# Weight chunks that begin at eight places in turn

## The chip, the cores and the metric

The kernel runs on one core of one Trainium2 chip. The metric is the device time in microseconds of one execution. Three runs of the kernel before took 3026.98, 3027.91 and 3037.3 us; the median is 3027.91 us.

## What is computed

Two transformer blocks of two layers each, one after the other, on 512 tokens of 1024 features; the first block has 256 context tokens beside them. All is in float32. In every layer the normalised input is multiplied by a wide input matrix, the products feed several mixers, and an output matrix closes the layer. Cut to what matters here, the first block is

```
h = rms_norm(x, g) * (1 + scale) + shift          # also for the context
qa, ka, va, za, qlb, kvlb, krb, zb, bc, cc, uc, zc, ga, gb, gc = split(h @ w_in)
ya = window_attention(qa, ka, va);  yb = latent_attention(qlb, kvlb, krb);  yc = bc * conv(cc * uc)
m  = sum over a, b, c of sigmoid(g) * ((y * silu(z)) @ w_branch)
x  = x + gate * rms_norm(m @ w_o, g_post)
```

and the second block

```
h = modulated rms_norm(x);  three mixers (attention, gated scan, attention) on split(h @ w_in)
x = x + gate * (mixers @ w_out)
h = modulated rms_norm(x);  u = conv(h @ w_up)     # 1024 -> 5632, 44 tiles of 128
x = x + gate * ((silu(u[:2816]) * u[2816:]) @ w_down)
```

## The kernel before

Features lie on the 128 partitions and tokens along the free dimension, so a feature tile is [128, 512] (with context [128, 768], as 512 and 256 columns). A matrix product runs tile by tile of its outputs: 128 output features at a time, over all feature tiles of the input.

Float32 products are made of two rounded parts: a number is a high part in float32r plus a low part in float32r, and `mm3` (line 174) adds up three products for each weight block of 128 x 128: high weights by high input, high weights by low input, low weights by high input. TensorE loads the block as its stationary operand and streams 512 or 256 columns of the input past it.

Weights come in chunks of 128 x 1024, eight blocks, through `wload` (line 149): SyncE issues the DMA of 512 KB into `wraw`, ScalarE casts it into the high part (`hi`, line 139), and VectorE subtracts to get the low part in pieces of 512 columns (`lo`, line 144). Most chunks go to the tiles `wh` and `wl`, two buffers of each, in the pool `wp`; these are the ones that the change touches:

```
h, l = (self.wp.tile([P, 1024], F32R, tag=t, name=self.nm(t), bufs=self.wb[1]) for t in ("wh", "wl"))
```

There are 364 of them. Chunks that have to stay longer, or that are loaded early, go to tiles of other pools (`w`, `mw`, `macc`, `w3`). In a chunk of 8 blocks of 128 columns block k lies 512 k bytes behind the chunk's start; in a chunk of 4 blocks of 256 columns 1024 k bytes.

The order of the work is that of the code, as a planner lays it out over the engines' queues; where a stream has gaps, steps of generators fill in (`Fill`). Names of outputs in the trace: `mm` the input projections, `pu` the branch products of the merge, `po` the output product of the first block, `up` and `dn` the second block's feed-forward (and `dn<-oh` its mixers' output product). Streamed tiles: `hh`, `hl` the normalised input (`ch`, `cl` its context columns), `yh`, `yl` the gated branches, `ah`, `al` the feed-forward's inner values, `oh`, `ol` the mixers' output.

Of the kernel before, what the change touches and what calls it, by code (L numbers as in the profile page):

```python
# [10 lines left out]
F32R = mybir.dt.float32r  # L11
# [5 lines left out]
P = 128  # L17
D = 1024
# [12 lines left out]
class Cat:  # L31
    """Column ranges of one feature tile kept in two tiles, split at column 512."""
# [10 lines left out]
class Pools:  # L43
    """Two pools as one: the tags named lie in the second."""
# [8 lines left out]
class Halves:  # L53
    """A chunk of weights in two tiles of 512 columns."""
# [13 lines left out]
class Fill:  # L68
    """Steps of generators, emitted a few at a time among the steps of another stream."""
# [34 lines left out]
class Kern:  # L104
    def __init__(self, ctx, tc, A):
        self.ctx, self.tc, self.nc, self.A = ctx, tc, tc.nc, A
        self.uid = 0
        self.ps = None
        self.fill = Fill()
# [39 lines left out]
    def wload(self, src, kt, n, tag=None):  # L149
        """A chunk [128, kt*n] of weights as an exact sum of two float32r parts."""  # L150
# [3 lines left out]
        if halves:  # L154
            h, l = (Halves([self.bp.tile([P, S], F32R, tag=tag, name=self.nm("w"), bufs=self.bb[tag]) for _ in range(2)], n) for _ in range(2))
        else:
            if tag:
                h, l = (self.bp.tile([P, 1024], F32R, tag=tag, name=self.nm(tag), bufs=self.bb[tag]) for _ in range(2))
            else:
                h, l = (self.wp.tile([P, 1024], F32R, tag=t, name=self.nm(t), bufs=self.wb[1]) for t in ("wh", "wl"))  # L160
# [13 lines left out]
    def mm3(self, ps, w, x, cols, n0=0, n1=P, ks=None, start=True, stop=True, o=0):  # L174
        """ps[n, t - o] += sum_k w[k][:, n] x[k][:, t] from split operands."""
# [9 lines left out]
    def seq(self, a, b):  # L185
        """Keeps b behind a in their engine's queue."""
        self.tc.add_manual_dep(b.ins, a.ins.name,
                               mybir.DependencyInfo(mybir.DependencyClass.NoSync, mybir.DependencyReason.DATA), reason="order")

    def after(self, ins):  # L190
        """Keeps ins behind the last product so far."""
# [3 lines left out]
    def rsqrt(self, v, n, inv, pool=True):  # L195
        """(v*inv + eps)^-0.5 of a small [128, n]: a first guess from the exponent, one step of third order, one of second."""
# [9 lines left out]
        # y * (15 - 10 a + 3 a^2) / 8  # L206
# [20 lines left out]
    def colsum(self, ps, a, nt):  # L227
        """ps[p, t] = sum over the partitions of a[:, t*128 + p]."""
# [3 lines left out]
    def rows(self, ps, r, nt):  # L232
        """ps[m, t*128 + p] = r[p, t] for every m."""
# [5 lines left out]
    def silu_cols(self, src, n, name, w):  # L239
        """[128, 8, w] with silu of n vectors in the first n columns, zeros elsewhere."""  # L240
# [13 lines left out]
    def mod_chunk(self, sc, n, wsrc, bias, layer, g, mt):  # L254
        """mt[:, 8g:8g+8, :] = 1024 outputs of s @ w + b for n vectors, on the tensor engine."""
# [12 lines left out]
    def mod_rows(self, ps, n, bias, g, mt):  # L268
        """Output 256j + c of vector r, in row 32j + r and column c of ps, to features on partitions, plus bias."""
# [6 lines left out]
        # feature g*1024 + j*256 + s*128 + p sits in column s*128 + j*32 + r  # L276
# [6 lines left out]
    def mod_steps(self, sc, n, wsrc, bias, layer, g, mt):  # L283
        """The same with the products on the vector engine; one step a 128 rows of w."""
# [19 lines left out]
    def mod_tile(self, name, bsrc, layer, nf, n):  # L304
        """Room for modulation vectors, and their biases."""
# [33 lines left out]
    def norm_part(self, xs, mod, g, c0, c1, j, ishift, iscale, dst, tmp=None, acc=None, sq="t"):  # L339
        """Columns c0:c1 of h = rms_norm(x, g) * (1 + scale) + shift, split into the tiles that dst(k) gives; mod  # L340
        [128, 24, n], of which column j. tmp(k): room for x times its gain, so that x itself is left intact; without it x is
        normalised in place, before the modulation is at hand. A step a feature tile."""
# [34 lines left out]
    def square(self, x, c0, c1, acc, tag="t"):  # L377
        """acc + x^2 of columns c0:c1, in a tile of its own."""
# [17 lines left out]
    def rms_rows(self, acc, w, inv):  # L396
        """(mean over the partitions' sum of acc + eps)^-0.5 of w columns, on every partition."""
# [14 lines left out]
    def h_x(self):  # L412
        """Room for h's first 512 columns: gives dst for norm_part."""
# [10 lines left out]
    def h_ctx(self):  # L424
        """The same for the columns from 512 on, of two feature tiles side by side."""
# [14 lines left out]
    def h_half(self, c):  # L440
        """The same for columns c*256 to (c+1)*256 of 512."""
# [11 lines left out]
    def norm_halves(self, mod, g, ishift, iscale, room):  # L453
        """h of self.x in two halves of the columns; room: makes tiles for x times its gain."""
# [13 lines left out]
    # tiles of w_in: qa 0-3 (x1 of two heads, x2 of both), ka 4, va 5, za 6-9, qlb 10-12, kvlb 13-14,  # L468
    # zb 15-18, bc 19-22, cc 23-26, uc 27-30, zc 31-34, ga 35-42, gb 43-50, gc 51-58
    def rope2(self, ps, tn):  # L470
        """Rotates the first 512 columns of rows x1 h0, x1 h1, x2 h0, x2 h1 (32 each); later columns pass through."""
# [13 lines left out]
    def a_kv(self, ps=None):  # L485
        """Keys of both groups with two copies of each part, and token-major values."""
# [23 lines left out]
    def a_q(self, p, tn, ps=None):  # L510
        """Queries of heads 2p, 2p+1: both rotary halves' high parts, then their low parts."""
# [15 lines left out]
    def pv_out(self, blocks, ecol, vst, y, row, q0):  # L527
        """y[row:row+64, q0:q0+256] = sum over key blocks of values times transposed weights, for two query tiles side by
        side in the array; blocks: [(key block, query tiles of the two)]."""
# [19 lines left out]
    def normalise(self, e, r):  # L549
        """e *= r, a factor a row."""  # L550
        self.nc.vector.tensor_scalar(e, e, r, None, op0=ALU.mult)  # L551

    def a_pair(self, h, q, i0, y):
        """Window attention of head h for query tiles i0, i0+1."""
# [41 lines left out]
    def ctx_pair(self, score, vst, y, row, scale, negmax, sink):  # L596
        """Attention of one head among the context tokens."""
# [34 lines left out]
    def attention(self, tn, conv):  # L632
        """Both attentions; projections that neither needs yet, and the gated convolution, fill in."""
# [61 lines left out]
    def latents(self, tn):  # L695
        """Queries of the first attention still to come, then the second's latents, rotary parts and first heads."""
# [7 lines left out]
        # keys and values  # L704
# [29 lines left out]
        # queries; their rms factor goes into the softmax's scale  # L734
# [25 lines left out]
        # shared rotary key: rows x1 x2 and, 32 further, x2 x1  # L760
# [12 lines left out]
        # rotary parts of all query heads, 16 rows a head  # L773
# [26 lines left out]
    def b_heads(self, tn, hp):  # L800
        """Q and K of heads 2hp, 2hp+1, unsplit: [96, T] with the rotary part in rows 64-95."""
# [30 lines left out]
    def b_vals(self, half):  # L832
        """Values of 4 heads, token-major: [128, 6, 2, 64] a pair of heads."""
# [73 lines left out]
    def gate(self, b, i, y, z0, tn):  # L907
        """y * silu(z), kept in DRAM until the merge."""
# [10 lines left out]
    def load_y(self, b, tn):  # L919
        """Split gated values of one branch."""  # L920
# [11 lines left out]
    def merge(self, bs, tn):  # L932
        """self.mh, self.ml = split sum over branches of sigmoid(g) * (y @ w_branch)."""
# [51 lines left out]
    def w_out(self, parts, mod, g_post, xsrc, tail):  # L985
        """x + gate * rms_norm(m @ w_o, g_post), in parts of the columns (first, last, column of mod); tail(i, xs) gives
        the steps that follow on part i, among which the next part's products run."""
# [31 lines left out]
    def post(self, os, xs, acc, c0, c1, behind):  # L1019
        """x += rms_norm(o) of columns c0:c1, acc the sums of o's squares."""  # L1020
# [29 lines left out]
    def block1(self):  # L1050
        """Both layers of the first block; the result is left in self.x, [128, 512] a feature tile, and the second block's
        first normalised input in self.hh, self.hl."""
# [99 lines left out]
    def next_h(self, i, xs, os, xd, mod, g):  # L1152
        """The second layer's normalised input; x itself goes to DRAM."""
# [26 lines left out]
    def cols2(self):  # L1180
        """The columns in one piece or, for the first products after a norm, in two."""
# [3 lines left out]
    def head_sums(self, st, sqs, ind, h0, nh):  # L1185
        """st[tok, t, h0:h0+nh] = sums of squares of nh heads, whose rows the columns of ind select."""
# [4 lines left out]
    def head_rows(self, r, h0, nh, rep):  # L1191
        """[128, 512] with r[tok, t, h] on the rep rows of each of the nh heads."""
# [7 lines left out]
    def values(self, ps, nh, name, tag="pt"):  # L1200
        """Token-major values of nh heads of 64: [128, 4, nh, 64]."""
# [10 lines left out]
    # tiles of w_in_2: A x1 of heads q0-3, A x1 of q4 q5 k0 k1, A x2 of both (0-3), av 4, bq 5-6, bff 7-8, bfb 9-10,  # L1212
    # bi 11-12, bg 13-14, cq 15-17, ck 18, cv 19
    def attn2_unit(self, q, ks, v, kv, soft, finish, y, row, i0):
        """Attention of one head for query tiles i0, i0+1 over all 512 tokens; soft(ps, i, j, e) leaves scores in e,
        finish(es) turns them to normalised weights."""
# [14 lines left out]
    def mix_done(self, i, y):  # L1231
        """Feature tile i of the mixers' output, split as soon as there is room beside the layer's input."""
# [8 lines left out]
    def room(self):  # L1241
        """The layer's input is not needed any longer."""
# [5 lines left out]
    def qk_split(self, q, t):  # L1248
        """The parts of the two heads of a tile of queries: high on the head's rows, low on the other's."""
# [9 lines left out]
    def k_split(self, k, t):  # L1259
        """High and low part of two heads' keys, each twice."""  # L1260
# [10 lines left out]
    def stats(self, ts):  # L1271
        """(mean square + eps)^-0.5 of the two heads of each tile: [128 tokens, 4, 2] a tile."""
# [8 lines left out]
    def a_prep(self):  # L1281
        """Queries and keys of the first mixer; the queries' rms factor goes into the softmax's scale."""
# [65 lines left out]
    def c_prep(self, tiles):  # L1348
        """Normalised queries, with the softmax's scale, or keys of the third mixer."""
# [20 lines left out]
    def stagger(*gens):  # L1370
        """The first steps of each generator run before the last one of the generator ahead of it."""
# [38 lines left out]
    def b_prep(self, pair):  # L1410
        """Of two heads: queries, values, and f, 1-f and log f, each [forward, backward], of the forget gates."""
# [455 lines left out]
```

## Time and profile before

| | |
|---|---|
| median of the runs | 3027.91 us |
| the profiled execution: its span, first to last instruction | 3026.6 us |
| TensorE products, busy | 2920.6 us (96%), 17920 |
| VectorE, ScalarE, GpSimd, busy | 1924.7, 1353.0, 261.5 us |
| mean granted TensorE clock, share of full speed | 0.986 |
| DMA | 331.76 MB, mean 110 GB/s |

The engines are named PE (TensorE's products), PEld (its weight loads), DVE (VectorE), ACT (ScalarE), POOL (GpSimd) and SP (SyncE). A product is pipelined: its duration reaches past the start of the next one, so the time that it takes out of a full stream is the distance of two starts. L182 is the line of `mm3` that issues the products.

### The profile page before, as it was taken

How to read it: one execution, taken by the hardware profiler on the slowest of the kernel's cores; microseconds unless marked ns; L12 is line 12 of the kernel's file. 1: busy time of each engine (PE TensorE's matmuls, PEld its weight loads, DVE VectorE, ACT ScalarE, POOL GpSimd, SP SyncE). 2: the span in 40 equal slices, each digit the busy share in tenths (PEclk: the TensorE clock that was granted, in tenths of full speed). 3: DMA queues.
4: the chain of work that ended last, by engine and by line, in shares of the span. 5: the costliest groups of instructions: out<-in, count | busy, mean ns of one | idle time of the engine just before them, and what ended most of it. 6: DMA issues, size and time to landing. Idle time of an engine off the chain costs nothing.

```text
span 3026.6 us, 46233 instructions
## 1 busy us (share of the span) xinstructions
PE 2920.6 (96%) x17920; PEld 2417.4 (80%) x17920; DVE 1924.7 (64%) x3720; ACT 1353.0 (45%) x2414; POOL 261.5 (9%) x520
## 2 busy tenths in 40 slices
PE   7999999999998999999998998999999998999999
PEld 4888888888887888777778876788888876788887
DVE  5666555555556566656676777688853778576642
ACT  3445544322234345653225775544433675554421
POOL 2000000001112000000112212000000223000000
PEclk9999999999998999999999999999999999999999
DMA  6221111333342423124653211355543311233232
GB/s 236 76 69 53 55 63 64 116 127 124 119 160 85 126 80 106 52 69 174 232 201 132 76 47 48 105 177 200 189 142 115 97 43 53 85 100 97 98 107 89
DMA packets 113163, 331.76 MB, mean 110 GB/s; under 512 B 18160, under 2 KB 20720, under 8 KB 112944
## 3 DMA queue, kind: packets, MB, share of 16 engines
q1 hardware_dynamic: 112944, 328.81, 33.6%
q8 instruction: 141, 2.31, 0.3%
q14 instruction: 78, 0.64, 0.1%
HBM read 300.51 MB, written 17.76 MB: 105 GB/s over the span
## 4 chain that ended last, share of the span: by engine, by line
PE 84%; DVE 8%; ACT 2%; DMA 2%; issue 2%; POOL 2%; SPq 0%; DVEq 0%; ACTq 0%; POOLq 0%
PE mm L182 32%; PE up L182 15%; PE dn L182 11%; PE pu L182 5%; PE pv L544 4%; PE pt L539 4%; PE po L182 2%; PE s L851 2%; PE s L568 1%; PE s L1223 1%; DVE zz L1527 1%; DVE wl L144 1%; PE pre L182 1%; PE pq L182 1%; DMA yg<-yd 1%
## 5 line engine op out<-in xcount | busy, mean ns | idle before, releaser
L144 DVE TENSOR_TENSOR wl<-wraw,wh 128x512 fp32r<-128x512 f32 (+2 forms) x706 | 473.1, 709 | 391.3 <-ACT wh L139 382.8
L139 ACT CAST wh<-wraw 128x1024 fp32r<-128x1024 f32 (+4 forms) x364 | 365.8, 1005 | 754.2 <-PE mm L182 241.5
L182 PE MATMUL mm<-hh,wh 128*128 128x512 f32 (+1 forms) x1240 | 488.8, 397 | 9.2 <-ACT hh L373 3.5
L182 PE MATMUL mm<-hl,wh 128*128 128x512 f32 (+1 forms) x1240 | 487.9, 394 | 5.0 <-DVE hl L374 5.0
L182 PE MATMUL mm<-hh,wl 128*128 128x512 f32 (+1 forms) x1240 | 487.3, 393 | 0.0
L182 PEld LDWEIGHTS mm<-hh,wh 128*128 128x128 f32 x1240 | 235.0, 191 | 58.2 <-ACT wh L139 6.9
L182 PEld LDWEIGHTS mm<-hl,wh 128*128 128x128 f32 x1240 | 235.8, 190 | 50.3 <-DVE hl L374 7.0
L182 PEld LDWEIGHTS mm<-hh,wl 128*128 128x128 f32 x1240 | 235.5, 190 | 49.6 <-DVE wl L144 3.0
L182 PE MATMUL up<-hh,wh 128*128 128x512 f32 (+1 forms) x688 | 261.1, 381 | 3.8 <-DVE fu L1643 2.3
L182 PE MATMUL up<-hl,wh 128*128 128x512 f32 (+1 forms) x688 | 261.0, 380 | 0.5
L182 PE MATMUL up<-hh,wl 128*128 128x512 f32 (+1 forms) x688 | 261.2, 380 | 0.2 <-DVE wl L144 0.2
L541 ACT COPY pT<-pt 128x512 f32<-128x512 f32 (+1 forms) x304 | 159.5, 551 | 177.0 <-PE pt L539 175.7
L294 DVE SCALAR_TENSOR_TENSOR macc<-mw,sc,macc 128x1024 f32<-128x1024 f32 x140 | 181.0, 1308 | 74.1 <-DMA mw<-w_mod 38.8
L539 PE MATMUL pt<-ident,E 128*128 128x128 f32 x1120 | 174.7, 282 | 4.1 <-DVE E L551 3.4
L539 PEld LDWEIGHTS pt<-ident,E 128*128 128x128 f32 x1120 | 127.8, 142 | 39.6 <-issue 24.4
L182 PEld LDWEIGHTS up<-hh,wh 128*128 128x128 f32 x688 | 128.8, 188 | 30.2 <-ACT ah L139 2.7
L182 PEld LDWEIGHTS up<-hl,wh 128*128 128x128 f32 x688 | 129.1, 188 | 26.2 <-DVE hl L374 1.3
L182 PEld LDWEIGHTS up<-hh,wl 128*128 128x128 f32 x688 | 129.1, 188 | 25.8 <-DVE wl L144 0.9
L964 POOL TENSOR_TENSOR m<-m,gt 128x768 f32<-128x768 f32 (+1 forms) x32 | 54.5, 1704 | 1077.4 <-DVE gt L960 755.8
L182 PE MATMUL mm<-ch,wl 128*128 128x256 f32 x504 | 143.7, 285 | 0.0
L182 PE MATMUL mm<-cl,wh 128*128 128x256 f32 x504 | 143.2, 284 | 0.0
L182 PE MATMUL mm<-ch,wh 128*128 128x256 f32 x504 | 143.1, 284 | 0.0
(416 smaller groups left out, 6135.7 us busy)
## 6 DMA issues: line engine op xcount, KB each, us to landing
wraw<-w_in SPq DMA_DIRECT2D x158, 512.0 KB, 3.5
mw<-w_ada SPq DMA_DIRECT2D x96, 512.0 KB, 4.4
wraw<-w_up SPq DMA_DIRECT2D x88, 512.0 KB, 3.5
mw<-w_mod SPq DMA_DIRECT2D x32, 512.0 KB, 3.5
wraw<-w_down SPq DMA_DIRECT2D x32, 512.0 KB, 3.5
wraw<-w_branch SPq DMA_DIRECT2D x24, 512.0 KB, 3.7
wraw<-w_out SPq DMA_DIRECT2D x22, 512.0 KB, 3.5
wraw<-w_o SPq DMA_DIRECT2D x19, 512.0 KB, 3.7
```

Of the source, the lines that this page charges most:

```text
L139: self.nc.scalar.copy(out, in_)
L144: (eng or self.nc.vector).tensor_tensor(out, in_, hi.bitcast(F32), op=ALU.subtract)
L182: self.last = self.nc.tensor.matmul(ps[: n1 - n0, c0 - o:c1 - o], lhsT=a[:, k, n0:n1], rhs=b[j][:, c0:c1], start=start and i == 0, stop=st ...
L294: nc.vector.scalar_tensor_tensor(acc[r], w, sc[:, k, r:r + 1], acc[r], op0=ALU.mult, op1=ALU.add)
L539: nc.tensor.transpose(pt[:, o * P:o * P + P], ecol(j, kb), self.ident)
L541: nc.scalar.copy(tt[:, :n], pt[:, :n])
L544: nc.tensor.matmul(pv[64 * j:64 * j + 64, :P], lhsT=vst(kb), rhs=tt[:, o * P:o * P + P], start=i == ends[j][0], stop=i == ends[j][-1])
L568: nc.tensor.matmul(s[:, c0:c1], lhsT=q[:, i * P:(i + 1) * P], rhs=kp[:, a0:a0 + c1 - c0], start=pi == 0, stop=pi == 1)
L851: self.nc.tensor.matmul(ps, lhsT=a[:96, i * P:(i + 1) * P], rhs=b[:96, c0:c1], start=pi == 0, stop=pi == 2)
L964: nc.gpsimd.tensor_tensor(ms[n][:, :tn], ms[n][:, :tn], m[:, :tn], op=ALU.add)
L1223: nc.tensor.matmul(s, lhsT=q[:, i * P:(i + 1) * P], rhs=kp, start=pi == 0, stop=pi == 1)
L1527: self.nc.vector.tensor_tensor(z[rows, h].rearrange("p (b u x) -> p b u x", u=2, x=H), q[rows].rearrange("p (b u x) -> p b u x", u=2, x=H) ...
```

## The change

The tiles `wh` and `wl` become 64 elements (256 bytes) longer. A counter goes round through 1 to 7 and 0, and a chunk begins 8 elements (32 bytes) times the counter behind its tile's start; both parts of a chunk have the same place. All that reads and writes the chunk goes by the slice. Chunks in other tiles stay as they were. Docstrings and comments are replaced by empty lines. The core of the diff:

```diff
@@ class Kern, __init__
-        self.uid = 0
+        self.uid, self.wturn = 0, 0
@@ wload
             if tag:
                 h, l = (self.bp.tile([P, 1024], F32R, tag=tag, name=self.nm(tag), bufs=self.bb[tag]) for _ in range(2))
             else:
-                h, l = (self.wp.tile([P, 1024], F32R, tag=t, name=self.nm(t), bufs=self.wb[1]) for t in ("wh", "wl"))
+
+                self.wturn = (self.wturn + 1) % 8
+                h, l = (self.wp.tile([P, 1024 + 64], F32R, tag=t, name=self.nm(t), bufs=self.wb[1])[:, 8 * self.wturn:8 * self.wturn + 1024]
+                        for t in ("wh", "wl"))
```

## Rows read from the trace of the kernel before

**Rows 1.** The page: span, busy time of each engine, the chain that ended last.
```profile
span 3026.6 us, 46233 instructions
...
PE 2920.6 (96%) x17920; PEld 2417.4 (80%) x17920; DVE 1924.7 (64%) x3720; ACT 1353.0 (45%) x2414; POOL 261.5 (9%) x520
...
PE 84%; DVE 8%; ACT 2%; DMA 2%; issue 2%; POOL 2%; SPq 0%; DVEq 0%; ACTq 0%; POOLq 0%
```

**Rows 2.** Waits of TensorE: waiter, waited for, us in total, times, longest.
```profile
PE mm L182 <- ACT wh L139: 3.3, 4, 1.0
...
PE po L182 <- DVE wl L144: 2.6, 1, 2.6
```

**Rows 3.** Products grouped by form: shape, count, busy us, mean ns, idle before.
```profile
L182 PE MATMUL mm<-hh,wh 128*128 128x512 f32 x1208 | 481.3, 400 | 8.1 <-ACT wh L139 3.3 <-ACT hh L373 2.4 <-DVE m L960 2.0
...
L182 PE MATMUL up<-hh,wl 128*128 128x512 f32 x624 | 243.5, 390 | 0.0
...
L182 PE MATMUL mm<-ch,wl 128*128 128x256 f32 x504 | 143.7, 285 | 0.0
...
L182 PE MATMUL dn<-ah,wl 128*128 128x512 f32 x330 | 130.2, 395 | 0.0
...
L182 PE MATMUL pu<-yl,wh 128*128 128x512 f32 x192 | 75.7, 394 | 0.0
...
L182 PE MATMUL dn<-oh,wl 128*128 128x256 f32 x160 | 45.4, 285 | 0.0
```

**Rows 4.** Timeline of TensorE in the up projection: start, us, first and last of seven.
```profile
2749.74 0.39 PE L182 MATMUL up<-hh,wl 128*128 128x512 f32 x1
...
2751.10 0.39 PE L182 MATMUL up<-hh,wl 128*128 128x512 f32 x1
```

**Rows 5.** The same in the down projection, first and last of seven.
```profile
2949.73 0.39 PE L182 MATMUL dn<-ah,wl 128*128 128x512 f32 x1
...
2951.13 0.39 PE L182 MATMUL dn<-ah,wl 128*128 128x512 f32 x1
```

**Rows 6.** Windows, two of up, one of down: us, PE busy (products), clock, DMA.
```profile
2700.00:2800.00 100.00, 100.00 (x443) 1.00 0.30 96
2800.00:2900.00 100.00, 100.00 (x442) 1.00 0.31 98
2910.00:3010.00 100.00, 100.00 (x430) 1.00 0.37 110
```

**Rows 7.** Timeline, 256 columns, mixers' output product, first and last of eight.
```profile
1932.75 0.28 PE L182 MATMUL dn<-oh,wh 128*128 128x256 f32 x1
...
1933.59 0.28 PE L182 MATMUL dn<-ol,wh 128*128 128x256 f32 x1
```

**Rows 8.** Timeline, 256 columns, weights in w, first and last of nine.
```profile
1975.86 0.28 PE L182 MATMUL up<-hh,w 128*128 128x256 f32 x1
...
1976.77 0.28 PE L182 MATMUL up<-hh,w 128*128 128x256 f32 x1
```

**Rows 9.** Timeline, 256 columns, streamed tile mh, first and last of eleven.
```profile
1611.81 0.28 PE L182 MATMUL po<-mh,w 128*128 128x256 f32 x1
...
1613.00 0.28 PE L182 MATMUL po<-ml,w 128*128 128x256 f32 x1
```

**Rows 10.** Timeline: first and last product behind which a pitch was read.
```profile
47.70 0.39 PE L182 MATMUL mm<-hh,wh 128*128 128x512 f32 x1
...
2899.34 0.39 PE L182 MATMUL up<-hh,wl 128*128 128x512 f32 x1
```

**Rows 11.** Timeline behind a wait: first, eighth and eleventh of eleven products.
```profile
1421.62 0.39 PE L182 MATMUL mm<-hh,wh 128*128 128x512 f32 x1
...
1423.23 0.39 PE L182 MATMUL mm<-hl,wh 128*128 128x512 f32 x1
...
1423.91 0.39 PE L182 MATMUL mm<-hl,wh 128*128 128x512 f32 x1
```

**Rows 12.** The second block's attention scores by line: count, ns min/median/max, first, last.
```profile
L1223 PE MATMUL s<-kl,qa x96: 387/394/797, 1708.6 to 2600.8; 128*128 128x512 f32 x96
```

## The prediction

> **What bounds the kernel now.** I read the page first. TensorE is busy 2920.6 us of the span of 3026.6 us, and the chain that ended last is TensorE for 84% of the span, with the products of line 182 at its head [rows 1]. So a change matters here if it makes a product shorter or longer, or if it makes TensorE wait. The waits come next: the longest that TensorE has for the split of a weight chunk are a few us in total [rows 2]. ScalarE and VectorE split the chunks ahead of need, and what the change does to their writes has room. The grouped instructions show where the time is: three products a weight block, of 512 columns for the most part [rows 3].
>
> The reader is then to look at the pitch, from start to start of two products, and not at the duration, for products overlap. In the up projection of the second layer six pitches of 512 columns take 2751.10 - 2749.74 = 1.36 us, 226.7 ns each [rows 4]. In the down projection six take 2951.13 - 2949.73 = 1.40 us, 233.3 ns [rows 5]. Both streams run with no gap, at a granted clock of 1.00, the upper level of 2.4 GHz, and the counts of whole windows agree: 442 or 443 products in 100 us against 430 [rows 6]. At that clock 512 columns at one a cycle would be 213.3 ns (an estimate from the clock); so 13.3 ns a product are lost in the one and 20 ns in the other.
>
> The two stretches are the same code with the same weight tiles. What differs is where the streamed tile lies. In the compiled kernel before, the weight tiles begin at multiples of 4096 bytes of a partition and their blocks follow at 512 (or 1024) bytes; hh and hl begin at multiples of 2048; ah and al begin 64 bytes past a multiple of 128. While one product streams, the next weights are loaded beside it. I call the place of those weights less the place of the tile then streamed, modulo 128 bytes, the distance: 0 in the up projection, 64 in the down projection.
>
> Three more stretches speak of the distance. At 256 columns and distance 0, seven pitches take 0.84 us, 120 ns each [rows 7]. At 256 columns with weights 64 bytes off and the streamed tile aligned, eight take 0.91 us, 113.8 ns [rows 8]. At 256 columns with the streamed tile 96 past (distance 32), ten take 1.19 us, 119 ns, with single ones between 115 and 123 [rows 9]. So weights off by 64 helped a short product and a streamed tile off by 64 hurt a long one: the place matters, and its sign isn't the same for both lengths.
>
> **The change, part by part.** It adds no instruction, DMA, wait or queue step. It gives each chunk in wh and wl a start 32 times 0 to 7 bytes into its tile, so that the distance of its products runs through 0, 32, 64, 96 and again. The tiles grow by 256 bytes, four of them, 1024 bytes a partition; tiles behind them move by that, a multiple of 128, and keep their distance to everything else. Chunks in other tiles (w, mw, macc, w3) stay.
>
> First term, 512 columns at distance 0. Counted are mm 3 x 1208, up 3 x 624 and pu 3 x 192, together 6072 [rows 3]. The timeline's starts give 6053 pitches of such products under 250 ns, the first at 47.70 us and the last at 2899.34 us [rows 10]: mean 228.0 ns, 78% of them at 226 to 228. The others stand behind a wait: there seven pitches take 1423.23 - 1421.62 = 1.61 us, 230 ns each, before the pitch settles at 0.68 / 3 = 226.7 [rows 11]. Three of four chunks leave distance 0: 0.75 x 6053 = 4540 products.
> - At 64 I take 233.3, as in the down projection.
> - At 32 and 96 no steady stretch of 512 columns exists. From below: 220.0, one step of 6.7 ns under 226.7, as the short product gained (120 to 113.3). From above: 240.0, a step over 233.3. The nearest row is the attention's second product, whose streamed tile lies 64 past and whose weights 96 past: its median duration is 394 ns [rows 12], as long as a product of the down projection (394 to 395) and longer than one of the up projection (390) [rows 3]. Unsettled pitches behind a wait are 230. I take 232.5.
> - Mean of the three: 232.8. Cost 4540 x 4.8 ns = 21.8 us; ends 4540 x (224.4 - 228.0) = -16 us and 4540 x (237.8 - 228.0) = +44 us.
>
> Second term, the down projection: 3 x 330 = 990 products at distance 64 [rows 3]. A quarter comes to distance 0 and gains 6.7 ns (-1.7 us), half goes to 32 or 96 (-0.4 us at 232.5). Together -2 us; ends -8 and +2.
>
> Third term, 256 columns: ch and cl 3 x 504, oh and ol 3 x 160, together 1992 [rows 3]; three quarters, 1494, leave distance 0. At 120 now; 113.8 at 64 and 119 at 32 and, taken alike, 96: 117.3 on average, 2.7 ns less, -4 us; ends -9 (all at 113.8) and 0.
>
> Fourth term: a stream that today stays settled from chunk to chunk is thrown out at each new place. The chunks that come to distance 0 settle anew; seven pitches 3.3 ns above 226.7 are 23 ns, for a quarter of some 360 chunks 2 us.
>
> Fifth term, writes: the cast into wh and the subtraction into wl begin at the same multiples of 32 bytes. Nothing that the trace shows depends on that; they stay hidden as long as TensorE's waits for them stay at a few us [rows 2]. Were each of 364 casts 0.05 us longer, it would be 18 us on ScalarE, busy 45% [rows 1]. I take 0.
>
> Sum: 21.8 - 2 - 4 + 2 = 17.8 us of TensorE. It stands idle 106 us in all (3026.6 - 2920.6), and where it waits for others a slower product uses up some of the wait; I take off a tenth: 16 us. The profiled execution's span of 3026.6 becomes 3042.6; the median of the runs is 3027.9, 1.3 us more than that span, so 3044.
>
> Here the Trainium skill speaks against any effect. Its page "SBUF — State Buffer", section "Who interferes with whom", gives TensorE two read ports, one for the streamed operand and one for weights, independent of each other, and says that TensorE never waits on anyone. By that rule the sum would be 0 and the time 3028; the 6.7 ns between the two projections at one clock would then have to come from the streamed tile alone, which is the second rival.
>
> **Rivals.**
> 1. Distances 32 and 96 cost no more than 0, or only half of the step: the first term is then 4540 x (228.9 - 228.0) = +4 us at 226.7, or 4540 x (231.1 - 228.0) = +14 at 230, and with the rest 3026 to 3038: no change that can be told. For it: at 256 columns distance 32 lies between 0 and 64. Against: the 394 ns of the attention.
> 2. Only the place of the streamed tile counts, and the place of the weights doesn't. The time stays 3028. For it: up and down differ in nothing but the streamed tile. Against: at 256 columns the streamed tile is aligned in both stretches, and weights moved by 64 changed 120 to 113.8.
> 3. Faster: the loss of 13.3 ns a product is itself a collision of two reads that start at the same place, and places apart remove it, as for the short products with moved weights. With 220.0 at 32 and 96 it is -16 - 8 - 9 + 2 = -31 us, some 2998. It decides for faster by 0.5% once the mean of the shifted distances is under about 227 ns. Against: the one steady stretch of 512 columns off distance 0 is slower.
> 4. Both odd distances cost a further step (240.0): +44 + 2 + 0 + 2 = 48 us, 3076.
>
> **How the numbers follow.** The forecast (232 to 234 at 32 and 96) has 0.48, rival 1 has 0.25, rival 2 has 0.12, rival 3 has 0.11, rival 4 has 0.04. The forecast's own range is 3036 to 3054, from 230.5 to 234.5 with a pass-through between 0.8 and 1; about a seventh of it lies under 3043, which is 0.5% over the time before, about what a measurement of this kernel can tell from no change. So slower 0.45, same 0.44, faster 0.11. The range of 8 in 10 reaches over the rivals 1 and 2 and a little into 3: 3012 to 3056.
>
> **What would show it.** Right: in the up projection the pitch alternates by chunk, a quarter at 226.7 and the rest at 232 or more; in the down projection a quarter falls to 226.7; the counts of 100 us windows come to about 432 in both; the granted clock and the order of the instructions are as before. Wrong: the up projection stays at 226.7 throughout (rival 2), or goes below it in some chunks (rival 3), or TensorE shows longer waits for wh and wl, which no term of mine has.

## The result and the profile after

Four runs of the changed kernel took 3045.05 to 3049.03 us, median 3047.75; the kernel before, run beside it, 3028.86. The ratio is 1.0058, with a 95% interval of 1.0045 to 1.0071: slower by about 0.6%, 18.9 us between the medians. The forecast was 3044. The profiled execution took 3049.03 us, its span is 3047.3 us, 20.7 us over that of before, at the same mean clock of 0.986.

The page after, with the lines that answer to [rows 1]:

```profile
span 3047.3 us, 46233 instructions
...
PE 2943.4 (97%) x17920; PEld 2417.1 (79%) x17920; DVE 1925.1 (63%) x3720; ACT 1351.0 (44%) x2414; POOL 261.7 (9%) x520
...
PE 84%; DVE 8%; ACT 2%; DMA 2%; issue 2%; POOL 2%; SPq 0%; DVEq 0%; ACTq 0%; POOLq 0%
```

The count of instructions, the chain and the work of the other engines are as before; only TensorE is busy longer, by 22.8 us. Lines of the code lie three further down, so L182 is now L185. The waits for split weights, against [rows 2]:

```profile
PE po L185 <- DVE wl L144: 2.6, 1, 2.6
...
PE mm L185 <- ACT wh L139: 2.3, 3, 1.0
```

They have not grown. The products grouped by form, against [rows 3]:

```profile
L185 PE MATMUL mm<-hh,wh 128*128 128x512 f32 x1208 | 485.6, 403 | 7.6 <-DVE m L963 2.5 <-ACT hh L376 2.4 <-ACT wh L139 2.3
...
L185 PE MATMUL up<-hh,wl 128*128 128x512 f32 x624 | 246.5, 395 | 0.0
...
L185 PE MATMUL mm<-ch,wl 128*128 128x256 f32 x504 | 142.7, 283 | 0.0
...
L185 PE MATMUL dn<-ah,wl 128*128 128x512 f32 x330 | 130.3, 395 | 0.0
```

Up takes 395 ns a product instead of 390, mm 403 instead of 400, the down projection 395 as before, and 256 columns 283 instead of 285. Windows of 100 us, two of up and one of down (us, PE busy and products, clock, DMA), against [rows 6]:

```profile
2720.00:2820.00 100.00, 100.00 (x432) 1.00 0.29 95
2820.00:2920.00 100.00, 100.00 (x432) 1.00 0.29 94
2930.00:3030.00 100.00, 100.00 (x433) 1.00 0.35 111
```

The up projection fell from 443 to 432 products, the down projection rose from 430 to 433, all at a granted clock of 1.00. Next the timeline in the up projection, against [rows 4]: the first product of six chunks in a row, 24 products apart.

```profile
2742.61 0.39 PE L185 MATMUL up<-hh,wh 128*128 128x512 f32 x1
...
2748.21 0.40 PE L185 MATMUL up<-hh,wh 128*128 128x512 f32 x1
...
2753.72 0.40 PE L185 MATMUL up<-hh,wh 128*128 128x512 f32 x1
...
2759.31 0.39 PE L185 MATMUL up<-hh,wh 128*128 128x512 f32 x1
...
2764.76 0.39 PE L185 MATMUL up<-hh,wh 128*128 128x512 f32 x1
...
2770.35 0.40 PE L185 MATMUL up<-hh,wh 128*128 128x512 f32 x1
```

These chunks lie 160, 192, 224, 0 and 32 bytes into their tiles. Divided by 24 the steps are 233.3, 229.6, 232.9, 227.1 and 232.9 ns. So the pitch does change from chunk to chunk, as forecast; but one chunk of eight has the old pitch, not one of four, and the chunk at 192 has a value of its own, although 192 and 64 are the same modulo 128.

Over the whole kernel, with the starts of the trace and the places of the compiled program, the mean pitch of 512 columns by distance modulo 256 bytes is 228.1 (0), 233.0 (32), 233.3 (64), 233.8 (96), 232.5 (128), 233.3 (160), 229.8 (192) and 233.2 (224); 829 to 961 pitches stand behind each.

### The profile page after: what moved, and what is told of

The parts are those of the page before. It is cut to its first block, busy times and chain, and to the rows that moved or that the text cites. A ratio compares the mean times of both kernels' runs of the same rounds, so it can differ in the third digit from the quotient of the medians.

```text
span 3047.3 us, 46233 instructions
## 1 busy us (share of the span) xinstructions
PE 2943.4 (97%) x17920; PEld 2417.1 (79%) x17920; DVE 1925.1 (63%) x3720; ACT 1351.0 (44%) x2414; POOL 261.7 (9%) x520
## 4 chain that ended last, share of the span: by engine, by line
PE 84%; DVE 8%; ACT 2%; DMA 2%; issue 2%; POOL 2%; SPq 0%; DVEq 0%; ACTq 0%; POOLq 0%
PE mm L185 32%; PE up L185 16%; PE dn L185 10%; PE pu L185 5%; PE pv L547 4%; PE pt L542 4%; PE po L185 2%; PE s L854 2%; PE s L571 1%; PE s L1226 1%; DVE zz L1530 1%; DVE wl L144 1%; PE pq L185 1%; PE pk L185 1%; PE kr L185 1%
## 5 line engine op out<-in xcount | busy, mean ns | idle before, releaser
L185 PE MATMUL mm<-hh,wh 128*128 128x512 f32 (+1 forms) x1240 | 493.4, 401 | 8.6 <-ACT hh L376 3.5
L185 PE MATMUL mm<-hl,wh 128*128 128x512 f32 (+1 forms) x1240 | 492.8, 398 | 5.3 <-DVE hl L377 5.3
L185 PE MATMUL mm<-hh,wl 128*128 128x512 f32 (+1 forms) x1240 | 492.6, 398 | 0.0
L185 PEld LDWEIGHTS mm<-hh,wh 128*128 128x128 f32 x1240 | 235.4, 191 | 61.0 <-ACT wh L139 5.7
L185 PEld LDWEIGHTS mm<-hl,wh 128*128 128x128 f32 x1240 | 236.7, 191 | 54.1 <-DVE hl L377 6.8
L185 PEld LDWEIGHTS mm<-hh,wl 128*128 128x128 f32 x1240 | 236.4, 191 | 53.8 <-DVE wl L144 3.0
L185 PE MATMUL up<-hh,wh 128*128 128x512 f32 (+1 forms) x688 | 263.9, 385 | 2.3 <-ACT wh L139 1.1
L185 PE MATMUL up<-hl,wh 128*128 128x512 f32 (+1 forms) x688 | 264.0, 385 | 0.5
L185 PE MATMUL up<-hh,wl 128*128 128x512 f32 (+1 forms) x688 | 264.1, 385 | 0.0
L185 PEld LDWEIGHTS up<-hh,wh 128*128 128x128 f32 x688 | 128.8, 188 | 31.6 <-ACT hh L376 1.6
L185 PEld LDWEIGHTS up<-hl,wh 128*128 128x128 f32 x688 | 129.1, 188 | 29.5 <-DVE hl L377 1.3
L185 PEld LDWEIGHTS up<-hh,wl 128*128 128x128 f32 x688 | 129.1, 188 | 28.2 <-issue 0.8
L185 PE MATMUL mm<-ch,wl 128*128 128x256 f32 x504 | 142.7, 283 | 0.0
L185 PE MATMUL mm<-ch,wh 128*128 128x256 f32 x504 | 142.4, 283 | 0.0
L185 PE MATMUL mm<-cl,wh 128*128 128x256 f32 x504 | 142.3, 282 | 0.0
```

The costliest lines, as they stand in the source:

```text
L185: self.last = self.nc.tensor.matmul(ps[: n1 - n0, c0 - o:c1 - o], lhsT=a[:, k, n0:n1], rhs=b[j][:, c0:c1], start=start and i == 0, stop=st ...
```

## The experiments

**The pitch by itself.** A small kernel without the network, of bare products: 48 products in a row for each pair of places, in the order of `mm3`. The weights lie w bytes and the streamed tile x bytes behind the starts of their tiles. In the compiled program all these starts lie 128 bytes past a multiple of 256, so w less x is the distance modulo 256; the places themselves are 128 bytes off from those of wh, wl, hh and hl in the big kernel, which begin at multiples of 256. The core of the edit (places are in elements of 4 bytes):

```diff
+    for n in (512, 256):
+        for d in range(0, 32, 2):
+            run(f"w{4 * d:03d}x000n{n}c", n, d, 0)
+        for wp, xp in ((0, 16), (16, 16), (8, 8), (0, 8), (0, 24), (0, 0), (32, 0), (0, 32)):
+            run(f"w{4 * wp:03d}x{4 * xp:03d}n{n}e", n, wp, xp)
```

> A kernel of its own: no network, only streams of 48 products of 128x128 weights, three a weight block as in the big kernel, at chosen places of the weights (w, bytes) and of the streamed tile (x, bytes), 512 and 256 columns; its output isn't the reference's. Theory D (the distance of the next weights from the streamed tile, modulo 128 bytes, sets the pitch): at 512 columns 226.7 ns at w000x000, w064x064, w032x032, w128x000 and w000x128; 233.3 at w000x064 and w064x000; between 231 and 235 at distances 32 and 96; at 256 columns 120 at distance 0, 113.3 to 117.7 at 64, about 118.4 at 32 and 96. Theory A (only the streamed tile's place counts): all w...x000 alike at 226.7, and w064x064 and w000x064 alike at 233.3. Theory W (only the weights' place counts): w064x064 like w064x000.

Timeline of this kernel; each name holds w, x and the columns, and of each pair stand the 18th and the 48th product, 30 pitches apart. The granted clock is 1.00 throughout (20 to 400 us):

```profile
27.76 0.39 PE L36 MATMUL w000x000n512c<-xha,wla 128*128 128x512 f32 x1
...
34.56 0.39 PE L36 MATMUL w000x000n512c<-xha,wla 128*128 128x512 f32 x1
...
71.61 0.40 PE L36 MATMUL w032x000n512c<-xha,wla 128*128 128x512 f32 x1
...
78.61 0.40 PE L36 MATMUL w032x000n512c<-xha,wla 128*128 128x512 f32 x1
...
194.67 0.39 PE L36 MATMUL w120x000n512c<-xha,wla 128*128 128x512 f32 x1
...
201.47 0.39 PE L36 MATMUL w120x000n512c<-xha,wla 128*128 128x512 f32 x1
...
216.57 0.39 PE L36 MATMUL w064x064n512e<-xha,wla 128*128 128x512 f32 x1
...
223.37 0.40 PE L36 MATMUL w064x064n512e<-xha,wla 128*128 128x512 f32 x1
...
271.78 0.39 PE L36 MATMUL w128x000n512e<-xha,wla 128*128 128x512 f32 x1
...
278.74 0.40 PE L36 MATMUL w128x000n512e<-xha,wla 128*128 128x512 f32 x1
```

That is 6.80 us / 30 = 226.7 ns at distance 0, 7.00 / 30 = 233.3 at 32, 226.7 at 120, 226.7 with both 64 off, and 6.96 / 30 = 232 at 128. The other steps of 8 bytes lie between 230.0 and 234.3; weights at 0 with the streamed tile at 64 give 228.9. Two things follow. The streamed tile at 0 gives 226.7 or 233.3 by where the weights lie, so rival 2 of the prediction is false; and with both moved alike the pitch is that of distance 0, so it is the difference of the two that counts. Distance 0 gives 226.7 here as in the big kernel, though both places are 128 bytes off from there. And 128 is not 0: the prediction's modulo 128 is false.

At 256 columns the same scan runs from 113.3 (at 64 and 88) over 120.0 (at 0) to 121.7 (at 24):

```profile
292.16 0.28 PE L36 MATMUL w000x000n256c<-xha,wla 128*128 128x256 f32 x1
...
295.76 0.28 PE L36 MATMUL w000x000n256c<-xha,wla 128*128 128x256 f32 x1
...
337.59 0.28 PE L36 MATMUL w064x000n256c<-xha,wla 128*128 128x256 f32 x1
...
340.99 0.28 PE L36 MATMUL w064x000n256c<-xha,wla 128*128 128x256 f32 x1
```

**The longer tiles alone.** All chunks at 0, the tiles 256 bytes longer.

```diff
-  self.wp.tile([P, 1024], F32R, ...)
+  o = 0; ... self.wp.tile([P, 1024 + 64], F32R, ...)[:, o:o + 1024]
```

> The tiles 256 bytes longer, every chunk at the tile's start. Theory D: no change, 3028 us within 0.2%. Theory L (the longer tiles, and what they move behind them by 1024 bytes, cost the time): 3047 us.

3030.02 against 3030.98 us, ratio 0.9995 (0.9985 to 1.0004). An up window and a down window:

```profile
2800.00:2900.00 100.00, 100.00 (x443) 1.00 0.29 96
2910.00:3010.00 100.00, 100.00 (x430) 1.00 0.36 108
```

Both counts are those of the kernel before. Length and layout are not the cause.

**All chunks at 64 bytes.** One place, no turns.

```diff
+  o = 16; ... self.wp.tile([P, 1024 + 64], F32R, ...)[:, o:o + 1024]
```

> Longer tiles, every chunk 64 bytes into its tile. Theory D: the steady up projection goes to 233.3 ns a product and the down projection to 226.7; 6053 x (233.3 - 228.0) = +32 us, 990 x 6.7 = -6.6, 256 columns 1994 x -4.5 = -9, a tenth off for waits: +15, 3043 us. Theory A: no change, 3028. Theory W (weights off by 64 cost in themselves): up and down both at 233.3 or more, 3050 to 3060.

3048.81 us, ratio 1.0057 (1.004 to 1.0074), as slow as the change. The same two windows:

```profile
2800.00:2900.00 100.00, 100.00 (x430) 1.00 0.29 95
2910.00:3010.00 100.00, 100.00 (x430) 1.00 0.35 105
```

With a fixed place the up projection settles at the pitch that the down projection had. So the place costs, not its changing. The down projection kept 232.9 ns where modulo 128 promised 226.7: ah lies 192 bytes past a multiple of 256, and weights at 64 are then 128 off. By itself this run is also close to theory W, that weights off by 64 cost wherever the streamed tile lies; against W stand the bare products with both places moved alike, by 64 above and by 192 in the second scan below, at 226.7 each. The mean of all 512-column products but the down projection's went from 228.0 to 233.1, that of 256 columns from 118.9 to 116.0: 6053 x 5.1 - 3553 x 2.9 = +21 us, and the span rose by 20.1 (3046.7 - 3026.6).

**Places 128 and 0 in turn.**

```diff
+  o = 32 * (self.wturn % 2); ...[:, o:o + 1024]
```

> Longer tiles, chunks in turn at 128 and 0 bytes. Theory D (modulo 128): distance 0 throughout, 3028 us, the up projection at 226.7. If the period is longer than 128 bytes, or if it is the change of place from chunk to chunk that costs (theory T), slower: up projection over 229 and 3035 us or more.

3043.57 us, ratio 1.0036 (1.0025 to 1.0047). The windows:

```profile
2800.00:2900.00 100.00, 100.00 (x437) 1.00 0.30 96
2910.00:3010.00 100.00, 100.00 (x435) 1.00 0.36 108
```

By distance the mean pitches are 228.6 at 0 and 232.5 at 128, and in the down projection 233.3 at 64 and 229.1 at 192. So a move by 128 is not neutral: the chunks at 128 are the slow ones, and the period is longer than 128. That the change of place costs nothing by itself is left to the next run.

**Places 256 and 0 in turn.**

```diff
+  o = 64 * (self.wturn % 2); ...[:, o:o + 1024]
```

> Chunks at 0 and 256 bytes in turn, in tiles 256 bytes longer. Theory D: both places are the same modulo 256, so 226.7 in the up projection and 233.3 in the down projection as before, 3028 to 3031, ratio 1.000. Rival T (the change of place itself costs, or the period is 512 or more): as with places 0 and 128, the other chunks at 232 to 234 in the up projection, +13 us, ratio 1.0035 to 1.005.

3029.17 against 3029.88 us, ratio 1.0002 (0.9993 to 1.001); the windows:

```profile
2800.00:2900.00 100.00, 100.00 (x443) 1.00 0.29 98
2910.00:3010.00 100.00, 100.00 (x431) 1.00 0.35 108
```

Places that differ by 256 are the same place, and changing place from chunk to chunk costs nothing by itself.

**The rest of the period.** The bare products again, weights from 128 to 280 off, and more pairs; the tiles are 256 bytes longer than in the first scan.

```diff
+        for d in range(32, 72, 2):
+            run(f"w{4 * d:03d}x000n{n}c", n, d, 0)
+        for wp, xp in ((64, 64), (0, 64), (32, 32), (48, 48), (48, 32), (0, 48), (0, 16), (16, 0)):
```

> The kernel of bare products again (its output isn't the reference's): weights from 128 to 284 bytes off, and pairs of places. Theory D, from the first scan: at 512 columns 232.4 at 128, 233.4 at 160, 228.9 at 192, 233.3 at 224, and from 256 on the first scan's values again (226.7 at 256, 230.7 at 264, 233.4 at 272); both at 256, or both at 128 or 192: 226.7; weights at 0 and the streamed tile at 256: 226.7. If the period is 512 or there is none: 232 to 234 at 256 too. If it is the absolute place of either: both at 128 differ from both at 0. At 256 columns: 120 at distance 0 and at 256, 118 to 119 at 128.

Timeline, again the 18th and the 48th product:

```profile
116.50 0.40 PE L36 MATMUL w192x000n512c<-xha,wla 128*128 128x512 f32 x1
...
123.50 0.40 PE L36 MATMUL w192x000n512c<-xha,wla 128*128 128x512 f32 x1
...
205.16 0.39 PE L36 MATMUL w256x000n512c<-xha,wla 128*128 128x512 f32 x1
...
211.96 0.39 PE L36 MATMUL w256x000n512c<-xha,wla 128*128 128x512 f32 x1
```

At 256 it is 226.7 again, and 264, 272 and 280 give 230.7, 233.3 and 230.0, as 8, 16 and 24 did; 216 is a third cheap place (226.7). But 192 gave 233.3 where 228.9 was expected, while 0 with 64, the same distance, gave 228.9 in both scans; and 64 gave 117.8 at 256 columns, 113.3 in the first scan. The distance alone did not fix the pitch here.

**The way in.** Six pairs, each entered behind products at distance 0 (first and third time), behind distance 32 (second) and behind a pause (fourth).

```diff
+            run(q + "pa", n, 0, 0);  run(q + "fa", n, wp, xp)
+            run(q + "pb", n, 8, 0);  run(q + "fb", n, wp, xp)
+            run(q + "pc", n, 0, 0);  run(q + "fc", n, wp, xp)
+            nc.scalar.copy(x[0], raw[:, 256:256 + 1152])
+            run(q + "fd", n, wp, xp)
```

> Bare products once more (the output isn't the reference's). Six pairs of places, each entered four ways: behind 48 settled products of distance 0, behind 48 of distance 32, behind those of distance 0 again, and behind a pause (a copy that TensorE has to wait for). Theory E (one distance has more than one settled rhythm, and the way in picks it): at 512 columns 192 and the streamed tile at 64 (both distance 192) settle at 228.9 by some ways in and at 233.3 by others, the same way gives the same rhythm again (first and third), and at 256 columns distance 64 settles at 113.3 or at 117.8. Rival P (each of the two places counts by itself, beside the difference): 192 with 0 settles at 233.3 by all four ways and 0 with 64 at 228.9 by all four. Distance 120 at 512 columns: 226.7 by all ways if the two cheap distances are alike; distance 128: 232.4.

Timeline of 192 with 0, the 18th and 48th product: 512 columns, then 256 columns by the first and the fourth way in:

```profile
39.06 0.39 PE L36 MATMUL w192x000n512fa<-xha,wla 128*128 128x512 f32 x1
...
45.93 0.40 PE L36 MATMUL w192x000n512fa<-xha,wla 128*128 128x512 f32 x1
...
504.77 0.28 PE L36 MATMUL w192x000n256fa<-xha,wla 128*128 128x256 f32 x1
...
508.17 0.28 PE L36 MATMUL w192x000n256fa<-xha,wla 128*128 128x256 f32 x1
...
534.18 0.28 PE L36 MATMUL w192x000n256fd<-xha,wla 128*128 128x256 f32 x1
...
537.71 0.28 PE L36 MATMUL w192x000n256fd<-xha,wla 128*128 128x256 f32 x1
```

At 512 columns distance 192 settles at 228.9 by all eight ways in (both pairs). So rival P is false, and theory E's 233.3 by some of these ways did not come either. The second scan gave 233.3 for the same pair at the same places, entered from 184, a way in that no other run has; that the way in made the difference is argued here, not shown. At 256 columns two lasting rhythms of one pair stand side by side in one run: 113.3 and 3.53 / 30 = 117.7 for one pair, and distance 64 likewise (weights at 64: 113.3 behind the pause, 117.8 by the three other ways; weights at 0 and the streamed tile at 192: 113.3 by all four). For 256 columns that leaves open whether the two places also count by themselves. Ways in behind the same products gave the same rhythm again each time. The pairs at 64, 128 and 120 did not depend on the way in at 512 columns (233.3, 232.2 and 226.7).

**The down projection at distance 0.** Its chunks begin at 192, where ah and al lie; all others at 0.

```diff
+                self.off = 48
                 w = self.wload(self.A["w_down_2"][self.l, n][:, k0 * P:k1 * P], ...)
+                self.off = 0
```

> Only the down projection's chunks begin 192 bytes into their tiles, all others at 0. ah and al lie 192 bytes past a multiple of 256. Theory D (the place of the weights less the place of the streamed tile counts, modulo 256 bytes): the down projection comes to distance 0 and falls from 233.3 to 226.7 ns a product, 990 x 6.6 = -6.5 us, ratio 0.998; the up projection stays at 226.7. Rival M (modulo 128, as in the prediction): 192 is 64 modulo 128, as is ah's place, so the same -6.5 us: this run doesn't tell D from M, the runs with 128 did. Rival A (weights at their own multiple of 256 are best, wherever the streamed tile lies): nothing gained in the down projection, 233 or more, ratio 1.000 or above. Rival T (a change of place from chunk to chunk costs by itself): at most 2 us more than before, for places change only twice a layer.

3020.79 against 3029.88 us, ratio 0.9971 (0.9959 to 0.9982). The windows:

```profile
2800.00:2900.00 100.00, 100.00 (x443) 1.00 0.31 99
2910.00:3010.00 100.00, 100.00 (x443) 1.00 0.34 108
```

The down projection now runs at 443 products a window, 226.8 ns, and 982 pitches of 6.5 ns less are 6.4 us; TensorE is busy 2914.6 us, 6.0 less than before. Rival A, that weights do best at a multiple of 256 wherever the streamed tile lies, is false.

**Both lengths.** The same, and chunks used with 256 columns alone at 64: late chunks of the mixers' output product and the first two of the up projection.

```diff
+  self.off = 16; self.mm3(ps, self.wload(self.A["w_up_2"][self.l, j], KD, P, None if i < 2 else "act"), ...); self.off = 0
...
+  self.off = 0 if n < KD - 5 else 16; w = self.wload(A["w_out_2"][l, n], KD, P); self.off = 0
...
+  self.off = 16; w = late[n - KD + 5] if n >= KD - 2 else self.wload(A["w_out_2"][l, n], KD, P); self.off = 0
```

> The down projection's chunks at 192 bytes, and those chunks that are multiplied with 256 columns alone (late columns of the mixers' output product, first two chunks of the up projection) at 64 bytes, all others at 0. Theory D: -6.5 us in the down projection; the 256-column products of dn<-oh go from 120 to 113 to 115 ns: of 480, those of the late chunks, about -2 to -3 us; together -8 to -10 us, ratio about 0.997, below the kernel before by more than its uncertainty. Rival A: the 256-column gain alone, -2 to -3 us, ratio 0.999. If the passes saved are given back in waits of TensorE, the pitch falls and the time does not: ratio 0.999 to 1.000 with rows at 226.7.

3018.03 us, ratio 0.9966 (0.9953 to 0.9978): faster than the kernel before, and so than the changed one at 1.0058. It can't be told from the run before it by time: their intervals overlap, and TensorE is busy 2915.2 us against 2914.6 there. So a gain at 256 columns on top is not shown. At distance 64 its 256-column products average 116.6, not 113 to 115, for the pitches gather at both 113 and 118.

## Why the prediction came out right, step by step

- Pitch, not duration, and the difference of two places: right. The bare products show both, and the whole loss is busy time of TensorE: +22.8 us there, +20.7 in the span. That is 0.91 where 0.9 was taken, but no finer than one profiled execution of each allows: with the longer tiles alone, at the pitches of before, TensorE was busy 2925.1 us, 4.5 more.

```profile
PE 2925.1 (97%) x17920; PEld 2422.0 (80%) x17920; DVE 1926.9 (64%) x3720; ACT 1352.3 (45%) x2414; POOL 260.9 (9%) x520
```

- Modulo 128: wrong, it is 256. That left distance 0 to an eighth of the chunks, not a quarter. In place of 0.75 of the products at 232.8, seven eighths went to a mean of about 232.7 (the seven values above). The windows could not tell this: 432 was forecast for both projections, and 432 and 433 came.
- First and fourth term together, 21.8 + 2 = 23.8 us. The 512-column products outside the down projection went from a mean of 228.0 to 232.1: 6053 x 4.15 = 25.1 us. That it came out near is in part luck, for errors offset each other: more chunks left distance 0, but 192 (229.8) is much cheaper than the 233.3 taken for every 64. The 232.5 taken for 32 and 96 was 0.5 to 1.3 low (233.0 and 233.8). The fourth term's share was too large: the chunk at 0 above took 5.45 us for 24 products, 0.01 us more than 24 x 226.7 ns, where 0.023 us was taken, and only an eighth of the chunks pay it: under 0.5 us, not 2. The 6053, put down to mm, up and pu, take in the other 512-column products too, some 8% (by the starts 5544 pitches belong to those three and lead to another product of 512 columns).
- Second term, -2 us: the down projection's mean went from 233.3 to 232.0, 982 x -1.3 = -1.2 us. An eighth, not a quarter, is at the old pitch of up.
- Third term, -4 us: the mean over 256 columns went from 118.9 to 118.2; 3553 x -0.73 = -2.6 us. The 113.8 of [rows 8] is near one of two rhythms, and I took it as the price of the place. I also counted 1992 products where some 3100 of 256 columns read wh and wl; too few products and too high a gain offset each other.
- Fifth term, 0: right; the rows of waits have not grown and ScalarE is busy 1351.0 us against 1353.0.
- Sum: 25.1 - 1.2 - 2.6 = 21.3 us where 17.8 stood. The other 1.5 of TensorE's 22.8 us lie within the 4.5 us by which two executions with the same pitches differed.
- Rival 2 fails: 226.7 and 233.3 at one place of the streamed tile differ by the weights' place alone. The Trainium skill's page "SBUF — State Buffer", section "Who interferes with whom", calls TensorE's two read ports independent and says that TensorE never waits on anyone. The trace disagrees with what the prediction drew from that, a time of 3028: the weights' place alone made 6.7 ns a product.
- Rival 1 fails on 233.3 at 32, and rival 4 on the same number and on 233.8 at 96, where it had 240.0. Rival 3 fails at 512 columns, where no distance went under 226.6; for 256 columns places apart did help, and were worth 2.6 us.

Not shown is why. No row tells whether one of the two reads stands still, or which; the runs give the pitches and the period, not the mechanism.

## What to carry to other kernels

In a full stream of products, compare pitches between stretches of the same code; where they differ at one clock, look at the places of the two operands. What follows was measured with float32r products of 128 x 128 weights alone. Spreading places over the period takes the average (232 here); choosing them so that weights and streamed tile have the same place modulo 256 bytes took 512-column products to 226.7 and gave 0.3% (ratio 0.9971) without an instruction more. A period guessed from two places needs a scan: one cheap run of bare products would have told 128 from 256.

## What was unexpected of the hardware

- The period of 256 bytes, with cheap places for 512 columns at 0, 120 and 216 (226.7 ns) amid 228.3 to 234.3.
- The best places depend on the length: 256 columns are at 120.0 at distance 0 and reach 113.3 at 64, 88, 168 and 192.
- One pair of places can hold two lasting rhythms: weights at 192 gave 113.3 or 117.7 ns at 256 columns by the way in, in one run; at 512 columns they gave 228.9 in one run and 233.3 in another, and by what is not shown.
